# A residual made beside the first blocks and loaded back in the tail, and merge inputs by halves of tokens

## The chip, the cores and the metric

The kernel runs on one core of a Trainium2 chip. The metric is the device time of one execution in microseconds (us); the time quoted for a kernel is the median over its runs. A core has five engines with their own instruction lists: TensorE (PE, with its weight loads shown as PEld), VectorE (DVE), ScalarE (ACT), GpSimd (POOL) and SyncE (SP), which in this kernel only issues DMAs. SBUF is the on-chip memory, a bank is one of the eight PSUM banks into which TensorE writes.

## What is computed

One layer of a streaming encoder, all in fp32, for 1024 prompt tokens and 64 sample tokens (1088 in all) of width 1024. The rows of x are normalised, projected to 9864 columns, mixed by three branches (A: RWKV-7, B: mLSTM, C: stick-breaking attention), merged with gates, projected, normalised again and finished with a gated embedding. Cut to what matters here:

```python
x = layer_norm(x, ln_in_g, ln_in_b)
cols = x @ w_in + b_in
ys = stack([ya * silu(a_z), yb * silu(b_z), yc * silu(c_z)])
br = einsum('btnc,ncd->btnd', ys, w_branch)
mix = sum(sigmoid(gates) * br, axis=2) @ w_out
x = layer_norm(alpha * x + mix, ln_g, ln_b)      # alpha = 2 ** 0.25
x = x + (p @ w_ple) * sigmoid(x @ w_ple_gate)
```

The `alpha * x` of the last norm, with x the result of the first, is the residual that the change is about.

## The kernel before

Every fp32 operand of a large product is split into a high and a low part (`h`, `l`), and a product is three matmuls, h·h, h·l and l·h (`three`, called by `block`). Activations are kept transposed (channels on partitions, tokens along columns) in `xh` and `xl`, and the tokens come in three groups of 384, 384 and 320 columns.

**Stages.** `intro` loads nine tiles of x (128 tokens each, the last with 64), takes mean and variance of each row (`rs0`, `nmr0`), normalises the rows in place, and lets TensorE transpose them; the gain and bias `ln_in_g`, `ln_in_b` are applied to the transposed form. Its order is written out in the string `INTRO`. Then come the main blocks, one for each 128 columns of w_in: 8 pieces of the contraction x 3 matmuls x 3 token groups = 72 matmuls a block, some 12 us. The weights of a block are loaded by SP one or two blocks ahead (`wload`, L747) and split by ScalarE and VectorE one block ahead (`wsplit`; its subtraction reads the fp32 weights and their high part and shows as `whl<-heap,whl` of L358). At the end of a group VectorE and ScalarE empty the bank (`a_evac` for branch A: a shifted copy by ScalarE, one column of it by a POOL copy of L382, and a scalar-tensor step of VectorE). The three branches run as side tasks between these blocks. After the branches, `merge` multiplies their outputs with w_branch (its inputs, of 4 pieces, made by `yconv`: 4 x 3 matmuls for each of the three groups, 36 a block), and `tail` does the rest.

**What sets the order.** A planner, `Sched`, decides while the program is written out in which place of each engine's list an instruction stands. It keeps a simulated clock for each engine with costs given in `emit`, polls its tasks (lower priority numbers first) and puts a side task's instruction behind the main products that its clock says run until then. Each engine then executes its own list strictly in order and waits on semaphores. Side tasks are started with `S.spawn`.

**Branch A's front** (`a_front`, eight times, in two passes of 256 or 320 columns each) computes from three stored inputs the scaled keys and the norms of them. On VectorE it is a chain: tensor-scalar steps (L371), a scan (L401), products (L358) and scalar-tensor products (L376). At the end of a pass TensorE transposes the squares (`sq`) and multiplies with `bd`, a block-diagonal matrix of ones that sums over each head: the bd matmul. POOL's 128x128 memsets ahead of the fronts clear branch A's states.

**The tail.** For each of the nine token blocks TensorE does the products with w_out (8 pieces x 2 halves of 512 columns x 3 = 48 matmuls of 512 columns; 32 for the block of 64 tokens) and then, from the post norm `post`, 8 transposes of the normalised rows in two groups of 4. `post` on VectorE adds the residual tile to the two banks, takes statistics, and makes the normalised rows with two 128x1024 scalar-tensor steps (L376), between them a reciprocal square root by Newton steps on columns of 128x1. The residual tile comes from `res(t)`: SP loads x once more, POOL normalises it (L371) with `rs0` and `nmr0` and multiplies and adds two rows (L360) that `tail_rows` loaded on POOL's queue and VectorE scaled by alpha:

```python
yield self.dma(b, src, "s")
yield self.ts(b, b, self.rs0[:m, t:t + 1], OP.mult, nmr[:m, t:t + 1], OP.add, e="g")
yield self.tt(b, b, r3[:m, 0, :], OP.mult, "g")
yield self.tt(b, b, r3[:m, 1, :], OP.add, "g")
```

Beside this, VectorE splits the weights of the embedding (w_ple and w_ple_gate, loaded by SP; `heapr<-heap,heapr` 128x512 of L358), and the products of the embedding (`ple`) follow.

**The helpers' lines** in the profile: L321 a matmul, L328 a transpose on TensorE, L353 ScalarE, L358 and L360 a tensor-tensor step on VectorE and on POOL, L371 a tensor-scalar step, L376 a scalar-tensor-tensor step, L381 and L382 a copy on VectorE and on POOL, L401 the scan, L412 and L415 the statistics, L423 and L424 a memset on POOL and VectorE, L431 a DMA of a task, L747 the weight load. In the names, `heap` is the common SBUF pool (`heapr` the part that holds split operands), `bk` a bank, `pc` and `der` constants per channel.

## Time and profile before

| what | before |
|---|---|
| runs | 1802.21, 1797.72 and 1798.39 us, median 1798.39 |
| the profiled execution | 1793.48 us, its span 1791.5 us, granted TensorE clock 0.99 of full speed |
| TensorE busy | 1719.0 us (96% of the span), weight loads 1591.3 |
| VectorE busy | 1169.2 us (65%) |
| ScalarE busy | 790.8 us (44%) |
| POOL busy | 511.3 us (29%) |
| chain of work that ended last | TensorE 81%, VectorE 11%, ScalarE 4% |
| TensorE before its first product | some 33 us |
| longest waits of TensorE, whole run | transposes (L328) for VectorE L376: 22.1 us in 6; products (L321) for ScalarE L353: 15.0 us in 27; products for ScalarE's split in the merge: 5.7 us in 2 |

How to read it: busy time is the time in which an engine executed anything; an engine that is 96% busy leaves 72 us of the span. A line of a timeline gives the start, the duration, the engine, the line of the code, the operation, what is written from what, and in brackets the idle time of the engine just before it with what ended it. In a grouped line stand the count, the busy time, the mean duration in ns, and the idle time before these instructions. The runs without a profile lie 0.24 to 0.49% above the profiled execution.

### The profile page before, as it was taken

Reading aid. Unit: us, or ns where it says so; the run is one execution under the profiler, and the core shown is the slowest. Engines: PE = TensorE matmul, PEld = TensorE weight load, DVE = VectorE, ACT = ScalarE, POOL = GpSimd, SP = SyncE. Lnnn points to the kernel's source line nnn. Section 1 sums busy time; section 2 is a strip of 40 time slices with the busy share of each in tenths; the row PEclk is TensorE's granted clock in tenths of the full one; section 3 lists DMA queues with packets and bytes.
Section 4 is the critical chain, followed back from the end, with each engine's and each line's share of the span. In section 5 each row is a group of like instructions: output and inputs, shape, how many; then the busy total and the mean of one; then the engine's idle time right before and its main releaser. Section 6 shows DMA issues by size and latency. Waiting matters only on the chain.

```text
span 1791.5 us, 30062 instructions
## 1 busy us (share of the span) xinstructions
PE 1719.0 (96%) x10873; PEld 1591.3 (89%) x10873; DVE 1169.2 (65%) x2618; ACT 790.8 (44%) x1821; POOL 511.3 (29%) x1004
## 2 busy tenths in 40 slices
PE   6999999999999999999999999999998999978999
PEld 5999898888888999999999999999998999766787
DVE  8346567766766556777535757566664688888743
ACT  6444454445455455445436555554543223211421
POOL 6007554536645712321022112020210000354100
PEclk9999999999999999999999999999999999989999
DMA  5333331332332334543344342342326777321421
GB/s 156 100 102 93 96 103 54 111 104 67 94 103 72 91 106 147 160 138 122 114 128 141 98 121 94 90 130 71 109 64 193 240 254 232 129 71 59 143 83 53
DMA packets 223403, 207.64 MB, mean 116 GB/s; under 512 B 53396, under 2 KB 192454, under 8 KB 223254
## 3 DMA queue, kind: packets, MB, share of 16 engines
q1 hardware_dynamic: 195998, 163.99, 31.2%
q10 hardware_dynamic: 22552, 29.02, 4.5%
q0 software_dynamic: 4704, 12.71, 2.2%
q8 instruction: 85, 1.39, 0.3%
q14 instruction: 64, 0.52, 0.1%
HBM read 136.81 MB, written 68.90 MB: 115 GB/s over the span
## 4 chain that ended last, share of the span: by engine, by line
PE 81%; DVE 11%; ACT 4%; issue 2%; DMA 2%; ACTq 0%; SPq 0%; POOL 0%; DVEq 0%
PE bk L321 76%; PE bk L328 6%; DVE heap L376 4%; ACT heap L353 3%; DVE heap L358 2%; DVE heap L371 1%; DVE heapr L358 1%; DVE whl L358 1%; DVE heap L412 1%; DMA heap<-in_x_prompt_dram 1%; DVE xl L358 0%; DMA heap<-in_w_ple_dram 0%; DMA out_c_p_dram<-heap 0%; DVE heap L409 0%; ACT whl L353 0%
## 5 line engine op out<-in xcount | busy, mean ns | idle before, releaser
L321 PE MATMUL bk<-xh,whl 128*128 128x384 f32 (+3 forms) x3792 | 1056.7, 339 | 1.0 <-DVE xh L381 0.7
L321 PEld LDWEIGHTS bk<-xh,whl 128*128 128x128 f32 (+1 forms) x3792 | 681.1, 187 | 13.5 <-issue 3.9
L321 PE MATMUL bk<-xl,whl 128*128 128x384 f32 (+3 forms) x2184 | 669.2, 328 | 1.8 <-POOL xl L360 0.9
L321 PEld LDWEIGHTS bk<-xl,whl 128*128 128x128 f32 (+1 forms) x2184 | 404.0, 188 | 5.9 <-POOL xl L360 1.8
L353 ACT ACTIVATE heap<-bk 64x64 f32<-64x64 f32 (+9 forms) x679 | 219.2, 335 | 399.9 <-PE bk L321 137.8
L360 POOL TENSOR_TENSOR heap<-heap 32x30 f32<-32x30 f32 (+16 forms) x498 | 312.3, 627 | 37.3
L328 PE MATMUL bk<-ident,heap 128*128 128x128 f32 (+3 forms) x942 | 177.3, 280 | 36.4 <-DVE heap L376 22.1
L358 DVE TENSOR_TENSOR heap<-heap 128x256 f32<-128x256 f32 (+15 forms) x359 | 176.1, 497 | 16.2 <-DMA heap<-yz 7.8
L358 DVE TENSOR_TENSOR whl<-heap,whl 128x1024 fp32r<-128x1024 f32 (+1 forms) x114 | 121.7, 1069 | 91.2 <-ACT whl L353 87.9
L321 PE MATMUL bk<-heap 128*128 128x128 f32 (+6 forms) x1156 | 169.0, 270 | 10.0 <-ACT heap L353 8.5
L328 PEld LDWEIGHTS bk<-ident,heap 128*128 128x128 f32 (+3 forms) x942 | 120.7, 143 | 55.0 <-DVE heap L376 25.8
L321 PEld LDWEIGHTS bk<-heap 128*128 128x128 f32 (+2 forms) x1156 | 126.6, 163 | 40.6 <-ACT heap L353 21.9
L353 ACT ACTIVATE heap<-bk,pc 128x384 f32<-128x384 f32 (+5 forms) x218 | 114.1, 548 | 90.8 <-PE bk L321 69.2
L353 ACT ACTIVATE heap<-heap 64x64 f32<-64x64 f32 (+8 forms) x328 | 111.0, 343 | 63.4 <-DVE heap L376 30.5
L376 DVE SCALAR_TENSOR_TENSOR heap<-heap 128x4 f32<-128x4 f32 (+8 forms) x264 | 100.8, 383 | 55.3 <-ACT heap L353 49.6
L353 ACT ACTIVATE whl<-heap 128x1024 fp32r<-128x1024 f32 (+1 forms) x116 | 105.5, 911 | 70.7 <-PE bk L321 42.8
L401 DVE TENSOR_TENSOR_SCAN heap<-heap,cst 128x512 f32<-128x512 f32 (+8 forms) x68 | 96.4, 1419 | 45.5 <-POOL heap L418 26.1
L321 PE MATMUL bk<-heapr,whl 128*128 128x384 f32 (+2 forms) x648 | 117.2, 339 | 6.1 <-ACT heapr L353 5.7
L321 PEld LDWEIGHTS bk<-heapr,whl 128*128 128x128 f32 x648 | 110.2, 190 | 10.5 <-ACT heapr L353 6.3
L321 PE MATMUL bk<-heapr 128*128 128x256 f32 (+2 forms) x524 | 119.4, 329 | 0.0
L353 ACT ACTIVATE heap<-bk,hb 128x384 f32<-128x384 f32 (+1 forms) x120 | 67.7, 564 | 110.8 <-PE bk L321 87.8
L321 PE MATMUL bk<-heap,heap 128*128 128x128 f32 (+3 forms) x788 | 108.2, 263 | 8.3 <-ACT heap L353 6.5
(155 smaller groups left out, 1801.0 us busy)
## 6 DMA issues: line engine op xcount, KB each, us to landing
heap<-in_w_in_dram SPq DMA_DIRECT2D x77, 512.0 KB
heap<-gt SPq DMA_DIRECT2D x24, 544.0 KB
gt<-heap ACTq DMA_DIRECT2D x48, 192.0 KB
heap<-in_x_prompt_dram SPq DMA_DIRECT2D x16, 512.0 KB
heap<-crd SPq DMA_DIRECT2D x12, 544.0 KB
heap<-yd SPq DMA_DIRECT2D x24, 272.0 KB
heap<-yz SPq DMA_DIRECT2D x24, 272.0 KB
heap<-in_w_branch_dram SPq DMA_DIRECT2D x24, 256.0 KB
```

The costliest lines, as they stand in the source:

```text
L321: lambda: self.nc.tensor.matmul(out, lhsT, rhs, start=start, stop=stop, skip_group_check=more),
L328: lambda: self.nc.tensor.transpose(out, in_, self.ident[:p, :p]), load=(0.82 * fsize(in_), d))
L353: return self.nc.scalar.activation(out, in_, func, **kw)
L358: lambda: self.nc.vector.tensor_tensor(out=out, in0=a, in1=b, op=op))
L360: lambda: self.nc.gpsimd.tensor_tensor(out=out, in0=a, in1=b, op=op))
L371: lambda: q.tensor_scalar(out=out, in0=a, scalar1=s1, scalar2=s2, op0=op0, **kw))
L376: lambda: self.nc.vector.scalar_tensor_tensor(out=out, in0=a, scalar=s, in1=b, op0=op0, op1=op1))
L401: return self.S.emit("dve", fsize(out) * 2.13 + 90, rd, [out], lambda: self.nc.vector.tensor_tensor_scan(out=out, data0=d0, data1=d1, init ...
L412: return self.S.emit("dve", fsize(in_) * 1.06 + 65, [in_], [out], lambda: self.nc.vector.bn_stats(out=out, in_=in_))
```

## The change

A new task `resid` starts at the end of `intro` with priority 3. It keeps the nine tiles of normalised rows, loads `ln_in_g` and `ln_in_b` on SP, lets ScalarE scale them by alpha, and makes the residual in place with 18 POOL tensor-tensor steps; SP stores the nine tiles to DRAM (`resd`). In the tail `res` only loads such a tile, on SP; the second load of x, POOL's normalisation and its 18 steps there, two of the four rows and their scaling are gone. `yconv` converts the branch outputs in another order: the four pieces of the first 544 tokens first, then those of the second 544, for every merge (before: both halves of a piece, then the next piece). In `a_front` two memsets and one copy go from POOL to VectorE (24 small instructions in all).

```diff
--- before.py
+++ after.py
@@ -727,7 +727,24 @@
         for x in INTRO.split():
             if evs or x[0] not in "PEvW" and x[:2] != "w2":
                 f[x[0]](*(int(a) if a.isdigit() else a for a in x[1:]))
-        self.free(*xts, *tmps, bst)
+        self.free(*tmps, bst)
+        self.S.spawn(self.resid(xts), "resid", 3)
+
+    def resid(self, xts):
+
+        self.resd = self.dr.tile([9, 128, 1024], F32, name="resd")
+        R = yield from self.get(2048)
+        r3 = R.v(2, 1024)
+        for j, nm in enumerate(("ln_in_g", "ln_in_b")):
+            yield self.dma(r3[:, j, :], self.I[nm].rearrange("(a b) -> a b", a=1).to_broadcast([128, 1024]), "s")
+        for j in range(2):
+            yield self.act(r3[:, j, :], r3[:, j, :], AF.Copy, scale=2.0 ** 0.25)
+        for t, x in enumerate(xts):
+            m = 128 if t < 8 else 64
+            for j, op in enumerate((OP.mult, OP.add)):
+                yield self.tt(x[:m, :1024], x[:m, :1024], r3[:m, j, :], op, "g")
+            yield self.dma(self.resd[t, :m], x[:m, :1024], "s")
+        self.free(R, *xts)
 
 
     def wsetup(self, specs):
@@ -1022,7 +1039,7 @@
 
         h3, l3 = self.ys[n]
         H = NT // 2
-        it = [(k, slice(o, o + H)) for k in range(4) for o in (0, H)]
+        it = [(k, slice(o, o + H)) for o in (0, H) for k in range(4)]
         bs = []
         for _ in range(4):
             bs.append((yield from self.get(H)))
@@ -1115,13 +1132,10 @@
         self.wod = True
 
     def tail_rows(self):
-        rows = yield from self.get(4096)
-        r3 = rows.v(4, 1024)
-        for j, nm in enumerate(("ln_in_g", "ln_in_b", "ln_g", "ln_b")):
-            a = self.I[nm].rearrange("(a b) -> a b", a=1) if j < 2 else self.I[nm]
-            yield self.dma(r3[:, j, :], a.to_broadcast([128, 1024]))
-        for j in range(2):
-            yield self.ts(r3[:, j, :], r3[:, j, :], 2.0 ** 0.25, OP.mult)
+        rows = yield from self.get(2048)
+        r3 = rows.v(2, 1024)
+        for j, nm in enumerate(("ln_g", "ln_b")):
+            yield self.dma(r3[:, j, :], self.I[nm].to_broadcast([128, 1024]))
         self.rows = rows
 
     def tok(self, t):
@@ -1132,7 +1146,7 @@
         self.free(*self.Wr)
         self.banks += self.mbanks
         yield lambda: self.rows is not None
-        r3 = self.rows.v(4, 1024)
+        r3 = self.rows.v(2, 1024)
         mx = self.mix.v(8, NT)
         fl = lambda x: x.rearrange("p a b -> p (a b)")
         k3 = lambda x, c=128: x.rearrange("p (k c) -> p k c", c=c)
@@ -1146,18 +1160,13 @@
         hls = [[k3(wf[:, 2048 + 1024 * j:3072 + 1024 * j]) for j in range(2)]]
         hls += [[x[:, :, 512 + 128 * i:640 + 128 * i] for x in self.wo] for i in range(2)]
         self.x2d = self.dr.tile([9, 128, 1024], F32, name="x2d")
-        nmr = self.nmr0
         order = [0, 1, 2, 3, 4, 5, 6, 8, 7]
         sz = lambda t: 128 if t < 8 else 64
 
         def res(t):
-            m, src = self.tok(t)
+            m = sz(t)
             x = yield from self.get(1024)
-            b = x[:m, :1024]
-            yield self.dma(b, src, "s")
-            yield self.ts(b, b, self.rs0[:m, t:t + 1], OP.mult, nmr[:m, t:t + 1], OP.add, e="g")
-            yield self.tt(b, b, r3[:m, 0, :], OP.mult, "g")
-            yield self.tt(b, b, r3[:m, 1, :], OP.add, "g")
+            yield self.dma(x[:m, :1024], self.resd[t, :m], "s")
             self.res[t] = x
             if t < 8:
                 self.S.spawn(res(t + 1), "res")
@@ -1195,9 +1204,9 @@
                 yield self.bns(s[:m, 6 * h:6 * h + 6], r[:m, c])
                 self.unbank(bks[h])
             yield self.bna(s[:m, 12:14], s[:m, 0:12])
-            yield self.stt(r[:m, :1024], r[:m, :1024], s[:m, 12:13], r3[:m, 2, :], OP.subtract, OP.mult)
+            yield self.stt(r[:m, :1024], r[:m, :1024], s[:m, 12:13], r3[:m, 0, :], OP.subtract, OP.mult)
             yield from self.rsqrt(s[:m, 14:15], s[:m, 13:14], s[:m, 15:16], 1e-5)
-            yield self.stt(r[:m, :1024], r[:m, :1024], s[:m, 14:15], r3[:m, 3, :], OP.mult, OP.add)
+            yield self.stt(r[:m, :1024], r[:m, :1024], s[:m, 14:15], r3[:m, 1, :], OP.mult, OP.add)
             yield self.dma(self.x2d[t, :m], r[:m, :1024], "s")
             for k0 in (0, 4):
                 b = yield from self.bank()
@@ -1360,8 +1369,8 @@
         PC = yield from self.get(nc)
         bk3, kr3, pt3, ns3 = BK.v(nc, 128), KR.v(nc, 128), Pt.v(nc, 65), NS.v(nc, 2)
         nsb = NS[:, 2 * nc:3 * nc]
-        yield self.memset(pt3[:, :, 0], 1.0)
-        yield self.memset(ns3[64:128], 1.0)
+        yield self.memset(pt3[:, :, 0], 1.0, "v")
+        yield self.memset(ns3[64:128], 1.0, "v")
         yield
         w0, a0, kk, ka, rk = (self.pcol(n, p) for n in ("w0_a", "a0_a", "k_k", "k_a", "r_k"))
         lw = self.lw[:, p * 128:(p + 1) * 128]
@@ -1432,7 +1441,7 @@
             self.unbank(b1)
             self.unbank(b2)
             yield
-        yield self.cp(PC[:, :nc], pt3[:, :, 64], "g")
+        yield self.cp(PC[:, :nc], pt3[:, :, 64])
         self.free(*T, xk, xr, Pt)
         self.afdone = 2 * p + hf + 1
         self.S.note(f"   scores {p}{hf}")
```

Three places in the lists of the engines, before and after the change (a row that ends in x3 stands for three like instructions in a row; numbers of buffers are left out, and `heap_76` is a second part of the heap).

POOL, behind `intro`, beside the main blocks of branch A, before the change:

```order
L382 COPY heap<-der 128x1 x3
L423 MEMSET heap 128x128 x4
L423 MEMSET heap 128x1024
L382 COPY heap<-der 128x1 x4
L423 MEMSET heap 128x8
L423 MEMSET heap 64x16
L382 COPY heap<-der 128x1 x4
L382 COPY heap<-heap 128x8
```

And with the change:

```order
L423 MEMSET heap_76 128x1024
L360 TENSOR_TENSOR heap<-heap,heap_76 128x1024 x2
L382 COPY heap<-der 128x1 x2
L360 TENSOR_TENSOR heap<-heap,heap_76 128x1024 x5
L382 COPY heap<-der 128x1 x2
L360 TENSOR_TENSOR heap<-heap,heap_76 128x1024 x5
L382 COPY heap<-der 128x1 x2
L360 TENSOR_TENSOR heap<-heap,heap_76 128x1024 x4
L360 TENSOR_TENSOR heap<-heap,heap_76 64x1024
L382 COPY heap<-der 128x1 x2
L360 TENSOR_TENSOR heap<-heap,heap_76 64x1024
L382 COPY heap<-der 128x1 x4
```

The 18 steps now stand in one run behind the memsets, and between them only the one-column copies of the evacuations of two main blocks.

VectorE, the first pass of branch A's first front, before the change (ahead of these rows stand the tensor-scalar and the scan that begin the pass; the rows that read a bank or write `whl` belong to the main blocks):

```order
L371 TENSOR_SCALAR heap<-heap,der 128x256 x2
L358 TENSOR_TENSOR heap<-heap 128x256
L376 SCALAR_TENSOR_TENSOR heap<-bk_66,der,heap 128x384
L358 TENSOR_TENSOR heap<-heap 128x4x64 x2
L376 SCALAR_TENSOR_TENSOR heap<-heap,pc 128x2x128
L358 TENSOR_TENSOR heap<-heap 128x2x2x64
L376 SCALAR_TENSOR_TENSOR heap<-heap,pc 128x2x64
L376 SCALAR_TENSOR_TENSOR heap<-bk_67,der,heap 128x256
L376 SCALAR_TENSOR_TENSOR heap<-bk_67,der,heap 128x64
L376 SCALAR_TENSOR_TENSOR heap<-heap,pc 128x2x64
L358 TENSOR_TENSOR whl<-heap,whl 128x1024
```

And with the change, again behind that tensor-scalar and that scan:

```order
L371 TENSOR_SCALAR heap_76<-heap_76,der 128x256
L376 SCALAR_TENSOR_TENSOR heap<-bk_66,der,heap 128x384
L371 TENSOR_SCALAR heap_76<-heap_76,der 128x256
L358 TENSOR_TENSOR heap_76<-heap_76 128x256
L358 TENSOR_TENSOR heap_76<-heap_76 128x4x64 x2
L376 SCALAR_TENSOR_TENSOR heap_76<-heap_76,pc 128x2x128
L376 SCALAR_TENSOR_TENSOR heap<-bk_67,der,heap 128x256
L376 SCALAR_TENSOR_TENSOR heap<-bk_67,der,heap 128x64
L358 TENSOR_TENSOR whl<-heap,whl 128x1024
L376 SCALAR_TENSOR_TENSOR heap<-bk_65,der,heap 128x384
L358 TENSOR_TENSOR heap_76<-heap_76 128x2x2x64
L376 SCALAR_TENSOR_TENSOR heap_76<-heap_76,pc 128x2x64 x2
```

The evacuations and the weight split of the main blocks now stand ahead of the last three steps of the pass; on TensorE the transposes of the squares stand behind 402 main products instead of 366, and the bd matmul behind 405 instead of 375.

SP, the first loads of the tail, before the change:

```order
L431 DMA heap<-in_p_prompt_dram 128x256 x4
L431 DMA heap<-in_x_prompt_dram 128x1024
L431 DMA heap<-in_w_ple_dram 128x512 x2
L431 DMA heap<-in_p_prompt_dram 128x256 x2
L431 DMA heap<-in_w_ple_gate_dram 128x512 x2
L431 DMA heap<-in_x_prompt_dram 128x1024
L431 DMA heap<-in_w_ple_gate_dram 128x512 x4
L431 DMA x2d<-heap 128x1024
```

And with the change:

```order
L431 DMA heap<-in_p_prompt_dram 128x256 x4
L431 DMA heap<-in_w_ple_dram 128x512 x2
L431 DMA heap<-resd 128x1024 x2
L431 DMA heap<-in_p_prompt_dram 128x256
L431 DMA heap<-resd 128x1024 x2
L431 DMA heap<-in_p_prompt_dram 128x256
L431 DMA heap<-in_w_ple_gate_dram 128x512 x6
L431 DMA x2d<-heap 128x1024
L431 DMA heap<-resd 128x1024
```

Four tiles of the residual are loaded ahead of the first weights of the gate, where one tile of x stood. In TensorE's list of the tail the first transposes of the post norm stand behind 105, 147, 192, 237, 288, 333 and 386 products for blocks 0 to 6 (before: 120, 150, 216, 258, 291, 333 and 381), counted from the tail's first product.

## Rows read from the trace of the kernel before

**Rows 1.** (lines grouped by form, TensorE, 1524.2 to 1658.7 us): busy us, mean ns | idle before

```profile
L321 PE MATMUL bk<-xh,heapr 128*128 128x512 f32 x272 | 94.5, 415 | 0.0
L321 PE MATMUL bk<-xl,heapr 128*128 128x512 f32 x144 | 59.0, 410 | 0.0
L328 PE MATMUL bk<-ident,heap 128*128 128x128 f32 x60 | 12.6, 344 | 22.1 <-DVE heap L376 22.1
```

**Rows 2.** (timeline of TensorE, tail): start us, us, engine, line, op [idle before]

```profile
1540.23 0.39 PE L321 MATMUL bk<-xl,heapr 128*128 128x512 f32 x1
...
1551.90 0.39 PE L321 MATMUL bk<-xl,heapr 128*128 128x512 f32 x1
...
1556.54 1.12 PE L328 MATMUL bk<-ident,heap 128*128 128x128 f32 x4 [4.02 <-DVE heap L376]
...
1565.85 0.60 PE L328 MATMUL bk<-ident,heap 128*128 128x128 f32 x4
1566.20 0.48 PE L321 MATMUL bk<-xh,heapr 128*128 128x512 f32 x1
```

**Rows 3.** (windows): us, PE PEld DVE ACT POOL busy (x), PEclk, DMA share, GB/s

```profile
1582.00:1594.40 12.40, 5.98 (x20) 4.94 (x20) 11.81 (x23) 1.29 (x3) 4.20 (x2) 0.72 0.10 42
```

**Rows 4.** (lines grouped by form, POOL, 1500 to 1700 us)

```profile
L360 POOL TENSOR_TENSOR heap<-heap 128x1024 f32<-128x1024 f32 x16 | 42.7, 2671 | 1.3
...
L360 POOL TENSOR_TENSOR heap<-heap 64x1024 f32<-64x1024 f32 x2 | 4.9, 2434 | 0.2
```

**Rows 5.** (timeline of POOL: start of the run, and tail)

```profile
39.74 0.99 POOL L360 TENSOR_TENSOR xl<-heap,xh 128x320 fp32r<-128x320 f32 x1 [3.35 <-DVE xh L381]
...
1543.85 6.06 POOL L360 TENSOR_TENSOR heap<-heap 128x1024 f32<-128x1024 f32 x2
...
1599.09 5.14 POOL L360 TENSOR_TENSOR heap<-heap 128x1024 f32<-128x1024 f32 x2
```

**Rows 6.** (timeline of VectorE, tail)

```profile
1544.45 3.20 DVE L376 SCALAR_TENSOR_TENSOR heap<-heap 128x1024 f32<-128x1024 f32 x1
1547.57 2.89 DVE L358 TENSOR_TENSOR heapr<-heap,heapr 128x512 fp32r<-128x512 f32 x1
...
1550.94 0.16 DVE L376 SCALAR_TENSOR_TENSOR heap<-heap 128x1 f32<-128x1 f32 x1
...
1551.21 0.69 DVE L358 TENSOR_TENSOR heapr<-heap,heapr 128x512 fp32r<-128x512 f32 x1
...
1555.21 1.28 DVE L376 SCALAR_TENSOR_TENSOR heap<-heap 128x1024 f32<-128x1024 f32 x1
...
1601.75 0.68 DVE L358 TENSOR_TENSOR heap<-bk,heap 128x512 f32<-128x512 f32 x1
```

**Rows 7.** (timeline of SP's queue: the third weight load of the main blocks)

```profile
51.82 0.37 SPq L747 DMA_DIRECT2D heap<-in_w_in_dram  x1
```

**Rows 8.** (DMA issues, tail): out<-in, queue, count, KB each, us to landing

```profile
heap<-in_ln_in_b_dram POOLq DMA_DIRECT2D x1, 512.0 KB, 5.2
```

**Rows 9.** (timeline of ScalarE, start of the merge)

```profile
1382.95 0.66 ACT L353 ACTIVATE heapr<-heap 128x544 fp32r<-128x544 f32 x1 [1.75 <-DVE heap L376]
```

**Rows 10.** (timeline of VectorE: intro, and the first front of branch A)

```profile
39.04 0.55 DVE L381 CAST xh<-heap 128x320 fp32r<-128x320 f32 x2
39.91 1.00 DVE L381 CAST xh<-heap 128x320 fp32r<-128x320 f32 x1
...
83.94 0.30 DVE L371 TENSOR_SCALAR heap<-heap 128x256 f32<-128x256 f32 x1 [1.07 <-ACT heap L353]
...
91.40 0.34 DVE L376 SCALAR_TENSOR_TENSOR heap<-heap,pc 128x128 f32<-128x128 f32 x1
```

**Rows 11.** (timeline of TensorE, first front of branch A)

```profile
92.39 0.59 PE L321 MATMUL bk<-heap,bd 128*128 128x256 f32 x2
...
97.60 0.70 PE L321 MATMUL bk<-heap 64*128 64x256 f32 x4
```

**Rows 12.** (timeline of TensorE, start of the merge)

```profile
1381.26 0.69 PE L321 MATMUL bk<-heapr,whl 128*128 128x384 f32 x1 [5.06 <-ACT heapr L353]
```

## Prediction

> **What bounds the kernel now.** I read the busy times of the page first (the table ahead): TensorE is busy 1719.0 of 1791.5 us, so only about 72 us of the span can be won without taking products away. Then the waits of TensorE, to see where those 72 lie: the first 33 us (nothing loaded yet), some 20 us in small pieces inside branch A, 6 us where the merge begins, and the tail. The tail is the largest and the only one that one cause explains. From its first product at 1524.27 to the first product of the embedding at 1658.73 TensorE issues 272 + 144 = 416 products of 512 columns and 60 transposes, and the transposes stood waiting for VectorE for 22.1 us [rows 1]. The reader is to see in the timeline of TensorE what dense work costs there: between two like products at 1540.23 and 1551.90 lie 51 products, 0.229 us each, and four transposes take 0.35 us (1565.85 to 1566.20) [rows 2]. 416 x 0.229 + 60 x 0.0875 = 100.5 us; the stretch lasted 134.5. So 34.0 us are lost: 22.1 of waiting, 11.9 of slow running behind the waits, where four transposes take 1.12 us and not 0.60 (1556.54 against 1565.85) [rows 2]; the granted clock, 0.99 over the whole run (the table), is 0.72 over the longest wait and its wake [rows 3], a mean of the two levels 1.2 and 2.4 GHz.
>
> Why VectorE is late there: beside the chain of each block (residual add, statistics, two 1024-wide steps, Newton steps) POOL makes the residual: for each block a normalisation and two products of 128x1024, which took 2.67 us [rows 4]; a multiply and an add alike are called a product here. While a product runs, a VectorE instruction with two inputs in SBUF does not run: the 128x1024 step took 3.20 us and a 128x512 subtraction 2.89 us under the pair of products at 1543.85 [rows 5, 6], together 4.1 us over the 1.28 and 0.69 that they take at 1555.21 and 1551.21 [rows 6], and the transposes behind them waited 4.02 us [rows 2]. An add that reads a bank and one SBUF tile took 0.68 under the pair at 1599.09 [rows 5, 6]: it is not held. One such VectorE instruction gets through per POOL product, no more.
>
> **Part 1, the residual leaves the tail.** Removed there: nine x loads, 9 POOL normalisations, 18 POOL products, two row loads, two VectorE scalings. Added: nine loads of the stored residual on SP, of the same size. SP now has four of them ahead of the w_ple_gate loads (the order of SP, ahead), where one x tile stood before; 1.5 MB more ahead of the first gate weights is covered, since those weights are first used after product 416, some 90 us later. Without POOL all the holding goes. The change also has transposes earlier in TensorE's list (block 0 after 105 products instead of 120, block 2 after 192 instead of 216); the undisturbed chain of a block is some 8 us of VectorE time (four 512-wide steps at 0.7, two 1024-wide at 1.28, some fifteen small ones at 0.16 [rows 6]), two splits per block run between, and the transposes stand 45 to 57 products, 10 to 13 us, behind their block, so what is late next is VectorE by a little. I allow 3 us of new waits (0 at best; 12 if the earlier places and the splits of weights that share VectorE cost half of what was won). Gain: 34.0 - 3 = **31 us** (22 to 34).
>
> **Part 2, the residual is made early.** The same 18 products now run on POOL behind the first memsets. When: the two rows are loaded by SP behind the third weight load, issued at 51.82 [rows 7], and one store, so at about 52.6 and 53.0; landing took 5.2 us for such a row [rows 8], ACT takes 0.66 for 544 columns [rows 9], so about 1.1 for a row; the first product starts near 59.5. Bare, a product is 2.43 us, the 64-row form, which was hardly disturbed [rows 4]. By 84 nine are done, with two weight splits held by 2 us each; a split runs most of a block ahead of its use and has that room. Then VectorE comes to the first front of branch A. In the order of VectorE, ahead, twelve of its instructions, up to the last product for the bd matmul, are of the kind that shares with POOL: nine with two SBUF inputs (one scan, four products, three scalar-tensor products, one weight split) and three tensor-scalars from SBUF to SBUF. Before, this chain ran from 83.94 to 91.74 [rows 10]. Now each waits for the POOL product in hand. I follow the list: tensor-scalar at 86.6, scan 89.3, tensor-scalar 92.4, evacuation 92.7, tensor-scalar 95.3, products 98.0, 100.8 and 103.6, scalar-tensor product 106.2; then an evacuation, the weight split (POOL's next copy waits for VectorE here, so it is not held), an evacuation, and the last product and two scalar-tensor products under the last POOL product: done at about 112.6. TensorE's list has the bd matmul 30 products later than before, which is just behind the second pair of front products, 97.60 in the old trace (the old bd matmul stood at 92.39) [rows 11]; less the matmul itself that is 97.5. It waits 112.6 - 97.5 = 15.1 us, and runs slowly behind it; 11.9 us over six waits, most of it behind the four long ones, makes 2.5 for one. Cost: **17.6 us**.
>
> Does the kind without a second SBUF input, the tensor-scalar, wait at all? A cast of that kind, SBUF to SBUF, took 1.00 us with POOL's product of 39.74 beside it, two others together 0.55 [rows 5, 10], so I count it in. The Trainium skill ("SBUF — State Buffer", Who interferes with whom) says more: copies, casts and tensor-scalars can take both ports and are then held, instructions with at most one SBUF input outside that mode are not. The trace agrees on the cast and on the bank-reading add; no row shows a tensor-scalar of this size under a POOL product. Without the three the chain would end at 107.9, the wait be 10.4 and the cost 12.9: the low end by rows; at the very best POOL's products fall where TensorE has room and it is 2 us. The high end is the tail's own price for 18 such products, 34 us.
>
> What else moves early: nine 512 KB stores on SP. A store waits for its POOL product, and behind it in SP's list stand stores of branch A's inputs and the weight loads. By the times above SP is held 1 to 5 us, while a weight is loaded a block (72 products, some 12 us) before its split: covered. POOL's one-column copies for the evacuations stand behind up to five products, 12 us, which is the block by which they run ahead; if they come 2 us late, TensorE has two more banks, 8 us. 24 memsets and copies go from POOL to VectorE, 0.1 to 0.3 us each, under the cover of TensorE: nothing. The nine kept tiles and the two rows hold 11,264 columns of the heap longer, so buffers change places; TensorE's list runs equal again some 640 block products on and stays within two dozen products of the old one until the tail.
>
> **Part 3, halves.** Before, TensorE waited 5.06 us for the seventh piece and went on at 1381.26 [rows 12]. Now the first group needs pieces 1 to 4 and starts without a wait, but the second group straddles both halves and needs piece 8, whose ACT copy ran at 1382.95 to 1383.61 [rows 9], its subtraction to 1384.4. Old: 27 products of the first block behind 1381.26; new: 15 behind 1384.4. At 0.17 us each that is 1385.9 against 1386.9; at half speed 1390 against 1389.5. I take **-0.5 us** (-2 to +1).
>
> **Sum.** -31 + 17.6 - 0.5 = -13.9. The profiled execution took 1793.48 us, 1779.6 after; it lies 4.9 under the median of the three, 1798.39, so I give 1798.4 - 13.9 = **1784.5 us**. A measurement here can tell about 0.3%, 5.4 us, from no change.
>
> **Rivals.**
> *Early is nearly free* (22%): VectorE reaches the front after POOL is through, or the holding falls into TensorE's room. For: an evacuation that is late by less than two groups of TensorE costs nothing. Against: nine products are still left at 84, and the bd matmul waits for the chain itself. The early cost is then 2 to 9, the time 1768 to 1776.
> *The tail pays only in part* (16%): the chains of the blocks stay late, by the earlier places of the transposes, and 12 us of waits return; with the early cost as summed or somewhat larger the change is within 0.3%, 1793 to 1803. That no part works as said is in this case too; against it stands that each wait in the tail has a held VectorE step just ahead.
> *Slower* (11%): one mechanism, POOL's list itself. Its one-column copies wait for VectorE, VectorE waits for its products, and SP's weight loads stand behind the stores that wait for POOL. If this ring makes the last product end after about 134 and not 112, the bd matmul waits 36 us and the early cost passes the tail's gain: 1804 to 1812. Against: the ring closes only at one place (ahead of the last product), and 22 us of VectorE's time would have to go.
> *Forecast* (51%): early 10 to 22, tail 27 to 33: 1777 to 1793.
>
> Range: from 1768, the free early place with a full tail, to 1797, where the second rival is cut in its middle; about 6% lie below, 14% above. Faster by over 0.3%: 0.51 + 0.22 = 0.73; within: 0.16; slower: 0.11.
>
> **What would show it.** In the profile after: no POOL product behind 1500 and the waits of transposes for VectorE in the tail down from 22.1 to some 3; 18 POOL products from 59 to 112, two-input VectorE instructions of 2.5 to 3 us between 85 and 112; one wait of TensorE of 10 to 15 us near 98, at the bd matmul, with a low clock behind it; at the merge two or three short waits in place of 5.06. If that one wait is missing, the early step is wrong; if transposes still wait 10 us in the tail, the first.

## The result and the profile after

The changed kernel takes 1766.79 us (median of 4 runs, 1764.83 to 1767.26) against 1798.06 of the kernel before (4 runs of the same job): the ratio is 0.9822, 95% interval 0.9802 to 0.9842, so it is 31 us faster, and 17.7 us faster than the 1784.5 that I forecast, just outside the range. Its profiled execution took 1766.90 us, 26.6 less than that of before (1793.48). Lines of its page, the clock's line of the page of before, and TensorE's waits after:

```profile
span 1765.1 us, 30061 instructions
...
PE 1711.2 (97%) x10873; PEld 1587.3 (90%) x10873; DVE 1154.9 (65%) x2640; ACT 792.6 (45%) x1823; POOL 493.6 (28%) x969
...
PEclk9989999999999999999999999999999999999999
```

```profile
PEclk9999999999999999999999999999999999989999
```

```profile
PE bk L321 <- DVE heap L376: 14.6, 6, 11.8
PE bk L321 <- ACT heap L353: 14.2, 27, 1.6
PE bk L328 <- ACT heap L353: 12.1, 2, 10.4
PE bk L321 <- ACT heapr L353: 4.0, 3, 1.7
```

(Waits: us in total, times, longest.) The transposes' wait for VectorE, 22.1 us before, is gone from the list, and a new wait of 11.8 us stands at its head. The low digit of the granted clock has moved from the tail to the third of the 40 slices of the span, around 100 us.

**The tail.** Grouped lines of TensorE from the first product with w_out, 1532.01, to the first of the embedding, 1634.13, and one row of VectorE:

```profile
L321 PE MATMUL bk<-xh,heapr 128*128 128x512 f32 x272 | 89.3, 397 | 0.0
L321 PE MATMUL bk<-xl,heapr 128*128 128x512 f32 x144 | 56.6, 393 | 0.0
L328 PE MATMUL bk<-ident,heap 128*128 128x128 f32 x60 | 9.1, 272 | 0.0
```

```profile
1548.67 1.28 DVE L376 SCALAR_TENSOR_TENSOR heap<-heap 128x1024 f32<-128x1024 f32 x1
```

The same instructions as in [rows 1] now last 102.1 us where they took 134.3 (1524.41 to 1658.75), without any wait and at a granted clock of 1.00, before 0.91. The 128x1024 step that took 3.20 us under POOL's pair [rows 6] takes 1.28.

**The first front.** VectorE, POOL and TensorE (start, duration, engine, line, operation):

```profile
84.87 1.95 DVE L371 TENSOR_SCALAR heap<-heap 128x256 f32<-128x256 f32 x1 [1.98 <-ACT heap L353]
86.85 2.77 DVE L401 TENSOR_TENSOR_SCAN heap<-cmask,heap 128x256 f32<-128x256 f32 x1
89.54 2.45 DVE L371 TENSOR_SCALAR heap<-heap,der 128x256 f32<-128x256 f32 x1
91.92 0.61 DVE L376 SCALAR_TENSOR_TENSOR heap<-bk,der,heap 128x384 f32<-128x384 f32 x1
...
94.59 5.44 DVE L358 TENSOR_TENSOR heap<-heap 128x256 f32<-128x256 f32 x3
99.97 2.55 DVE L376 SCALAR_TENSOR_TENSOR heap<-heap,pc 128x256 f32<-128x256 f32 x1
...
106.25 0.41 DVE L358 TENSOR_TENSOR heap<-heap 128x256 f32<-128x256 f32 x1
106.70 2.71 DVE L376 SCALAR_TENSOR_TENSOR heap<-heap,pc 128x128 f32<-128x128 f32 x2
```

```profile
60.09 4.93 POOL L360 TENSOR_TENSOR heap<-heap,heap 128x1024 f32<-128x1024 f32 x2 [6.31 <-ACT heap L353]
...
92.11 12.60 POOL L360 TENSOR_TENSOR heap<-heap,heap 128x1024 f32<-128x1024 f32 x5
...
106.66 2.33 POOL L360 TENSOR_TENSOR heap<-heap,heap 64x1024 f32<-64x1024 f32 x1
```

```profile
109.46 1.22 PE L321 MATMUL bk<-heap,bd 128*128 128x256 f32 x2 [11.82 <-DVE heap L376]
```

Of the VectorE instructions that POOL holds, one gets through per POOL step. The exceptions are the first of the three products at 94.59, which took 0.41 us at the seam of two POOL steps, and the product at 106.25, which meets POOL's copies, 0.41. The evacuation at 91.92, which reads a bank, takes its usual 0.61. The weight split took 2.77 us here (103.03), 1.23 before.

**The start of the merge**, which answers to [rows 12]:

```profile
1380.87 2.43 PE L321 MATMUL bk<-heapr,whl 128*128 128x384 f32 x13
...
1385.27 0.45 PE L321 MATMUL bk<-heapr,whl 128*128 128x384 f32 x1 [1.18 <-ACT heapr L353]
...
1388.34 1.77 PE L321 MATMUL bk<-heapr,whl 128*128 128x384 f32 x3 [1.69 <-ACT heapr L353]
1391.21 2.04 PE L321 MATMUL bk<-heapr,whl 128*128 128x384 f32 x4 [1.10 <-ACT heapr L353]
```

The first group's 12 products run through; the second group waits for the pieces of the second half one by one, three short waits in place of 5.06 us.

**Along the run.** The start of the same TensorE product in both profiled executions, read from the two traces (main products are those with the columns of w_in, counted from the first):

```
after so many main products     before     after    difference
400                               97.2      96.4      -0.8
800                              175.5     190.3     +14.8
1200                             283.7     292.8      +9.1
2400                             630.9     639.4      +8.5
first product of the merge      1373.0    1380.9      +7.9
first product with w_out        1524.4    1532.0      +7.6
first product of the embedding  1658.8    1634.1     -24.6
last matmul, end                1787.1    1760.9     -26.2
```

So the kernel is 14.8 us late behind the early step, 5.7 of them come back between the main products 800 and 1200 and 1.2 more up to the merge, the tail gains 32.2, and the stretch behind it 1.5.

### The profile page after: what moved, and what is told of

It reads as the page before. It is cut to its first block, busy times and chain, and to the rows that moved or that the text cites. A ratio compares the mean times of both kernels' runs of the same rounds, so it can differ in the third digit from the quotient of the medians.

```text
span 1765.1 us, 30061 instructions
## 1 busy us (share of the span) xinstructions
PE 1711.2 (97%) x10873; PEld 1587.3 (90%) x10873; DVE 1154.9 (65%) x2640; ACT 792.6 (45%) x1823; POOL 493.6 (28%) x969
## 4 chain that ended last, share of the span: by engine, by line
PE 83%; DVE 9%; ACT 4%; issue 2%; DMA 1%; POOL 0%; ACTq 0%; SPq 0%; DVEq 0%; POOLq 0%
PE bk L321 78%; PE bk L328 5%; DVE heap L376 3%; ACT heap L353 3%; DVE heap L358 2%; DVE heap L371 2%; DVE whl L358 1%; DMA heap<-yz 1%; DMA heap<-in_x_prompt_dram 1%; ACT whl L353 0%; DVE heap L412 0%; DVE xl L358 0%; ACTq L431 0%; DVE heap L381 0%; DVE heap L409 0%
## 5 line engine op out<-in xcount | busy, mean ns | idle before, releaser
L321 PEld LDWEIGHTS bk<-xh,whl 128*128 128x128 f32 (+1 forms) x3792 | 682.1, 188 | 12.3 <-issue 3.4
L360 POOL TENSOR_TENSOR heap<-heap 32x30 f32<-32x30 f32 (+14 forms) x480 | 267.9, 558 | 36.3
L358 DVE TENSOR_TENSOR heap<-heap 128x256 f32<-128x256 f32 (+16 forms) x352 | 168.0, 483 | 11.8 <-DMA heap<-yz 3.4
L321 PE MATMUL bk<-heap 128*128 128x128 f32 (+7 forms) x886 | 157.6, 293 | 8.7 <-ACT heap L353 7.8
L321 PEld LDWEIGHTS bk<-heap 128*128 128x128 f32 (+3 forms) x886 | 117.8, 182 | 30.7 <-ACT heap L353 19.9
L353 ACT ACTIVATE heap<-heap 64x64 f32<-64x64 f32 (+10 forms) x330 | 113.1, 347 | 45.4 <-DVE heap L376 18.4
L321 PE MATMUL bk<-heap,heap 32*32 32x32 f32 (+3 forms) x1058 | 125.7, 244 | 6.9 <-ACT heap L353 6.4
L321 PEld LDWEIGHTS bk<-heap,heap 128*128 128x128 f32 (+2 forms) x1058 | 98.7, 152 | 31.7 <-ACT heap L353 17.6
L321 PEld LDWEIGHTS bk<-heapr,whl 128*128 128x128 f32 x648 | 110.0, 191 | 10.4 <-ACT heapr L353 5.1
```

What stands on the lines that cost most here:

```text
L321: lambda: self.nc.tensor.matmul(out, lhsT, rhs, start=start, stop=stop, skip_group_check=more),
L353: return self.nc.scalar.activation(out, in_, func, **kw)
L358: lambda: self.nc.vector.tensor_tensor(out=out, in0=a, in1=b, op=op))
L360: lambda: self.nc.gpsimd.tensor_tensor(out=out, in0=a, in1=b, op=op))
```

## The experiments

**The early steps left out, in place.** The kernel leaves out the 18 POOL steps; every other row of every list stays where it was.

```diff
-                           lambda: self.nc.gpsimd.tensor_tensor(out=out, in0=a, in1=b, op=op))
+                           lambda: e == "g" and self.nc.gpsimd.tensor_tensor(out=out, in0=a, in1=b, op=op))
...
-                yield self.tt(x[:m, :1024], x[:m, :1024], r3[:m, j, :], op, "g")
+                yield self.tt(x[:m, :1024], x[:m, :1024], r3[:m, j, :], op, "n")
```

> The changed kernel without the 18 early POOL steps; every other instruction keeps its place in its engine's list (the stored residual is the normalised x alone). Theory (POOL's steps hold VectorE, and only in the first front): the wait of 11.8 us at the bd matmul near 98 us is gone, the two-input VectorE steps there take 0.3 to 0.7 us instead of 2.5, and the time falls from 1766.8 by the whole 14.5 us by which the run with the change is late at 150 us, to about 1752. Rival 1 (a late TensorE is partly paid back inside branch A, since the branch's chains then stand ready: 6 us came back between 220 and 370 us): without the delay those 6 us are lost again, and the time is about 1758. Rival 2 (the stores and ScalarE's scaling cost, not the steps): the wait stays and the time is 1765 to 1768.

1754.04 us (1752.82 to 1755.47). The scan of the first front, and the bd matmul, now without a wait:

```profile
86.23 0.69 DVE L401 TENSOR_TENSOR_SCAN heap<-cmask,heap 128x256 f32<-128x256 f32 x1
```

```profile
98.51 0.59 PE L321 MATMUL bk<-heap,bd 128*128 128x256 f32 x2
```

Against the changed kernel it is 13.65 us ahead at main product 800, still 13.6 at 1200, 12.3 at 2000 and 11.4 at the end. So the steps alone make the loss, 13.65 us, and only some 2 us of it come back further on. The 5.7 us between 800 and 1200 are another thing: this kernel has no delay at all, stands 1.2 us behind the kernel before at product 800 and 4.5 ahead of it at 1200. Rival 1 falls for most of the 6 us, rival 2 altogether.

**The residual alone**, merge order and the 24 small instructions as before:

```diff
-        it = [(k, slice(o, o + H)) for o in (0, H) for k in range(4)]
+        it = [(k, slice(o, o + H)) for k in range(4) for o in (0, H)]
...
-        yield self.memset(pt3[:, :, 0], 1.0, "v")
-        yield self.memset(ns3[64:128], 1.0, "v")
+        yield self.memset(pt3[:, :, 0], 1.0)
+        yield self.memset(ns3[64:128], 1.0)
...
-        yield self.cp(PC[:, :nc], pt3[:, :, 64])
+        yield self.cp(PC[:, :nc], pt3[:, :, 64], "g")
```

> The changed kernel with the merge inputs in the old order and the 24 small instructions of the fronts back on POOL; TensorE's list is that of the change but for a few places. Theory (the 6 us that come back between 220 and 370 us come from the other order of branch A's work, which the new task causes): 1767, the halves worth 0.3 us. Rival (they come from the small instructions, which left POOL's list): 1772 to 1774.

1768.74 us (1767.77 to 1768.97). At product 1200 it stands 1.1 us ahead of the changed kernel, so the small instructions bring nothing; the 5.7 us come with the order of branch A's work that the new task causes. Between the first product of the merge and the first with w_out it takes 151.65 us, the changed kernel 151.14.

**Branch A's inverses left out in both kernels, in place.** Which work of the other order is it? In the kernel before, the front of VectorE at 259 to 275 us lies beside POOL's inverse, 60 dependent steps that grow from 32x30 to 32x240 and shrink again, the longest in its middle (a grouped line names the form of its first step alone; "32x30 and smaller" in the expectation below is a misreading of it). POOL up to 276 us and three of VectorE's steps there, in the kernel before:

```profile
254.55 21.72 POOL L360 TENSOR_TENSOR heap<-heap 32x30 f32<-32x30 f32 x33
```

```profile
262.52 1.31 DVE L358 TENSOR_TENSOR heap<-heap 128x256 f32<-128x256 f32 x2
...
268.91 0.76 DVE L376 SCALAR_TENSOR_TENSOR heap<-heap,pc,heap 128x128 f32<-128x128 f32 x1
```

And in the changed kernel, POOL up to 300 us:

```profile
273.67 26.36 POOL L360 TENSOR_TENSOR heap<-heap 32x30 f32<-32x30 f32 x38
```

```profile
275.71 0.43 DVE L358 TENSOR_TENSOR heap<-heap 128x256 f32<-128x256 f32 x1
...
280.12 0.34 DVE L376 SCALAR_TENSOR_TENSOR heap<-heap,pc,heap 128x128 f32<-128x128 f32 x1
```

In the kernel before POOL starts 5 us ahead of the front (its scan stands at 259.98), which so meets the middle of the inverse; with the change both start together (POOL at 273.67, the scan at 273.79), and the first steps of the inverse are the short ones. That lessens the holding and does not end it: the second 128x128 step (280.94) still takes 0.60 us, and from the scan to that step's end VectorE needs 10.4 us before (259.98 to 270.37) and 7.7 after (273.79 to 281.54). TensorE's waits beside it, before (200 to 290 us) and after (210 to 300):

```profile
PE bk L321 <- ACT heap L353: 2.6, 5, 1.1
PE bk L321 <- DVE heap L386: 1.4, 2, 0.9
PE bk L328 <- DVE heap L358: 1.1, 1, 1.1
PE bk L321 <- DVE heap L376: 1.0, 1, 1.0
```

```profile
PE bk L321 <- ACT heap L353: 3.3, 6, 1.4
PE bk L328 <- DVE heap L358: 0.6, 1, 0.6
PE bk L321 <- DVE heap L371: 0.3, 1, 0.3
PE bk L321 <- DVE heap L376: 0.2, 1, 0.2
```

The waits for VectorE fall from 3.5 to 1.1 us. From main product 800 to 1200, 740 matmuls in either kernel, TensorE waits 4.9 us before and 2.2 after and runs at a granted clock of 0.98 and 1.00: of the 5.7 us 2.7 are waits, the rest is slower running.

The cut, `IE = "g"` to `IE = "n"` with the line of the first diff, in both kernels:

> The kernel before without the 480 small POOL steps (32x30 and smaller) of branch A's inverses, every other instruction in its place (the branch's inverse is left out). To be read beside the same cut of the changed kernel. Theory (the 5.6 us that the changed order wins between the main products 800 and 1200 are VectorE steps of branch A's front that no longer lie under POOL's small steps): the 128x256 steps near 262 us take 0.4 us and not 0.65 to 1.3, this kernel is 5 us or more ahead of the kernel before at main product 1200 (283.7 us), and the run with the change and this cut is 14 to 15 us behind this one there. Rival (the order wins it in another way, without POOL): the difference to the run with the change stays 9 us at product 1200.

> The changed kernel with the same cut, the 480 small POOL steps of the inverses left out in place. Theory: it loses 14 to 15 us against the cut kernel before up to main product 600 and still is 14 to 15 us behind at product 1200, so nothing comes back; its time is that of the cut kernel before less about 20 us. Rival: 9 us behind at product 1200, and the time less 25 us.

1770.60 us (2 runs) and 1750.37 (2 runs). Main product 1200 starts at 274.7 in the first, 9.0 ahead of the kernel before, and the difference between the two cut kernels is 13.8 us at product 800, 13.5 at 1200, 13.6 at 2400, 13.1 at the merge: next to nothing comes back. The time differs by 20.2 us. The theory holds. The same steps of VectorE in the cut kernel before:

```profile
259.05 0.76 DVE L358 TENSOR_TENSOR heap<-heap 128x256 f32<-128x256 f32 x2
...
262.69 0.34 DVE L376 SCALAR_TENSOR_TENSOR heap<-heap,pc,heap 128x128 f32<-128x128 f32 x1
```

It also leaves out the inverses' own time: TensorE's waits between 140 and 620 us fall from some 20 us to 5.1, and which part of that is holding was not separated. What the two cuts show is that the 5.7 us hang on the inverses.

**The tail's steps left out of the kernel before, in place** (`"n"` with the line of the first diff).

```diff
-            yield self.tt(b, b, r3[:m, 0, :], OP.mult, "g")
-            yield self.tt(b, b, r3[:m, 1, :], OP.add, "g")
+            yield self.tt(b, b, r3[:m, 0, :], OP.mult, "n")
+            yield self.tt(b, b, r3[:m, 1, :], OP.add, "n")
```

> The kernel before without the 18 POOL steps of the tail; loads, POOL's normalisation and all other places stay (the residual is the normalised x alone). Theory (the steps hold VectorE, nothing else in the tail matters): the transposes' waits for VectorE fall from 22.1 us to under 4, the half-speed stretches of the tail go, and the time is 1798 - 30, about 1768. Rival (the transposes' place in TensorE's list, or the loads of x and the normalisation, carry a good part): 8 us or more of waits stay, and the time is 1777 to 1790.

1760.84 us (1760.60 to 1761.42). With w_out it takes 102.3 us, the changed kernel 102.1. The loads of x and POOL's normalisations are still there, and no transpose waits:

```profile
L328 PE MATMUL bk<-ident,heap 128*128 128x128 f32 x61 | 9.5, 273 | 0.0
```

```profile
L371 POOL TENSOR_SCALAR heap<-heap,rs,nmr 128x1024 f32<-128x1024 f32 x8 | 12.2, 1522 | 73.6 <-DMA heap<-in_x_prompt_dram 55.0 <-DMA heap<-in_w_ple_dram 13.2 <-DVE heap L371 5.3
```

So the 18 steps are the whole loss of the tail; removing the loads and the normalisations, and the transposes' new places, give nothing that shows in the time. It came out 7 us under what I expected, 5 of them since the kernel before took 1793.22 us (13 runs) beside it and not 1798: to that the difference is 32.4 us, ratio 0.9826, interval 0.9800 to 0.9852.

**The kernel before once more.**

> The kernel before, profiled once more. Theory (the 4.9 us by which its profiled execution lay under the median are chance of that execution): the new profiled execution lies within 3 us of the median of the runs, 1795 to 1801, and the difference to the old one is in the tail's waits. Rival (a profiled execution of this kernel is some 5 us shorter always): 1791 to 1795 again.

1792.20 us over 10 runs, 1787.11 to 1800.00, the profiled one 1795.90, now 3.7 us above the median. A difference in the tail's waits was expected and did not show: 22.4 us beside 22.1. The 4.9 us were chance. The two profiles of the kernel before differ behind the tail, from the first product of the embedding to the last matmul: 128.3 us at a granted clock of 1.00 in the first, 131.3 at 0.97 in the second. The kernel before spreads over 13 us in these 10 runs, the kernel without POOL's tail steps over 0.8 in 4.

**The steps on VectorE.** First by the task's own call, so that the planner counts them there:

```diff
-                yield self.tt(x[:m, :1024], x[:m, :1024], r3[:m, j, :], op, "g")
+                yield self.tt(x[:m, :1024], x[:m, :1024], r3[:m, j, :], op)
```

> The changed kernel with the 18 early steps on VectorE instead of POOL. A 128x1024 step with two inputs takes VectorE 1.28 us where nothing holds it: 23 us in all, beside 10 of its 40 us in use between 45 and 84 us. Theory (only the holding by POOL costs, VectorE has room): the wait at the first bd matmul falls from 11.8 us to under 3, and the time lies between that without the steps, 1754, and 1760, so 7 to 12 us under the changed kernel. Rival (VectorE itself becomes late for the first front, some 8 of the steps stand among its work, or the other order of branch A loses its 5 us): 1762 to 1768.

1771.20 us (1769.82 to 1773.06), 4 more than the changed kernel and outside both ranges. At product 800 it is 14.4 us ahead of it, as hoped; at the first product of the merge 9.1 ahead, at the first with w_out 3.2 behind. The planner has another order, by which branch C ends later: TensorE is ahead and branch C is not. SP's queue stores its last output at 1365.60 us and the merge begins at 1371.78, 6.2 us later; in the changed kernel 1363.09 and 1380.87. The loads of the merge's inputs stand behind that store in SP's list, and TensorE waits for ScalarE's copies of them (9.8 us in 7, the changed kernel 4.0 in 3):

```profile
1365.60 0.45 SPq L431 DMA_DIRECT2D yd<-heap  x1
1366.21 0.46 SPq L431 DMA_DIRECT2D heap<-yd  x1
```

```profile
PE bk L321 <- ACT heapr L353: 9.8, 7, 2.3
```

Then by the planner's old count, so that the lists of TensorE, ScalarE and SP are the change's:

```diff
-                           lambda: self.nc.gpsimd.tensor_tensor(out=out, in0=a, in1=b, op=op))
+                           lambda: (self.nc.gpsimd if e == "g" else self.nc.vector).tensor_tensor(out=out, in0=a, in1=b, op=op))
...
-                yield self.tt(x[:m, :1024], x[:m, :1024], r3[:m, j, :], op, "g")
+                yield self.tt(x[:m, :1024], x[:m, :1024], r3[:m, j, :], op, "p")
```

> The changed kernel with the 18 early steps given to VectorE in the places at which they were called for POOL: the lists of TensorE, ScalarE and SP are those of the change to the last row, VectorE's has 18 rows more, POOL's 18 fewer. Five of them (1.28 us each) stand inside the first front's chain up to the last product for the bd matmul, eleven ahead of it. Theory (the cost of the early steps is POOL's holding, and the version on VectorE before lost its gain at the merge by another order of branch C): the wait at the first bd matmul is under 4 us, the merge begins as in the change, and the time is 1754 to 1759. Rival (VectorE has no room in the first front): the wait stays above 8 us and the time is 1762 or more.

1753.23 us (1753.09 to 1754.49), as fast as without the steps; the changed kernel took 1767.36 beside it. VectorE and the bd matmul (L360 is the line of POOL's call, here given to VectorE):

```profile
85.62 0.69 DVE L401 TENSOR_TENSOR_SCAN heap<-cmask,heap 128x256 f32<-128x256 f32 x1
...
88.03 1.22 DVE L360 TENSOR_TENSOR heap<-heap,heap 128x1024 f32<-128x1024 f32 x1
89.17 0.88 DVE L358 TENSOR_TENSOR heap<-heap 128x256 f32<-128x256 f32 x2
```

```profile
97.70 0.70 PE L321 MATMUL bk<-heap,bd 128*128 128x256 f32 x2
```

A step costs VectorE 1.22 us; waiting for one of POOL's cost an instruction of this chain some 2 us (the scan 2.77 instead of 0.69). The wait at the bd matmul is gone.

**A third pair of buffers for the merge's inputs**, on top of that:

```diff
-        for _ in range(4):
+        for _ in range(6):
...
-        yield from load_y(0)
+        for i in range(2):
+            yield from load_y(i)
...
-            if i < 7:
-                yield from load_y(i + 1)
+            if i < 6:
+                yield from load_y(i + 2)
```

(and `i % 3` for `i % 2` in the choice of a pair.)

> As the version with the 18 steps in place on VectorE, and the merge's inputs loaded through three pairs of buffers instead of two, so two pieces ahead. Theory (at the start of the merge each piece waits for its load, which waits for a buffer that the piece two before it gives free: the order of the halves moves the waits, the depth removes them): TensorE's waits for ScalarE at the merge, 4.0 us in 3, and the 6.8 us at half speed behind them fall to under half, and the time is 4 to 7 us below that version. Rival (the loads are bound by the DMA engines or by the last store of branch C, not by the buffers): within 2 us of that version.

1751.82 us (1751.40 to 1754.04): 2.1 us of the merge gained in the profiled execution, 1.4 in the medians. That is the rival's size, not the 4 to 7 us of the theory. The waits for ScalarE there, 4.2 us in 3 without the third pair:

```profile
PE bk L321 <- ACT heapr L353: 2.6, 3, 1.1
```

The depth takes a third of the waits and not all; what holds the rest was not followed. Its median is the lowest here, 0.977 of the kernel before, interval 0.9749 to 0.9792, but its runs and interval overlap with those of the version before it (0.9756 to 0.9798).

**The halves alone.**

```diff
-        it = [(k, slice(o, o + H)) for k in range(4) for o in (0, H)]
+        it = [(k, slice(o, o + H)) for o in (0, H) for k in range(4)]
```

> The kernel before with the merge's inputs by halves of tokens and nothing else. Theory: between the first product of the merge and the first with w_out TensorE needs 0.3 to 0.6 us less, two or three waits in place of the one of 5.06 us; the time cannot be told from that of the kernel before. Rival (three short waits cost more than a long one by the clock): 1 us or more longer in that stretch.

1795.64 us against 1794.18, ratio 1.001 (0.999 to 1.003). From the first product of the merge to the first with w_out it takes 151.44 us, the kernel before 151.43 and, in its second profile, 151.79. The waits are as foreseen, three short ones in place of one, and the gain is 0 to 0.5 us (the 0.5 from the residual alone, 151.65, to the whole change, 151.14): too small to tell.

**The inverses on VectorE**, `IE = "v"` in the changed kernel:

> The changed kernel with the 480 small steps of the inverses on VectorE instead of POOL. Theory (POOL's small steps hold VectorE longer than VectorE would take for them): TensorE's waits between 140 and 620 us, 16.5 us in the changed kernel, fall by a third or more, 1757 to 1763. Rival (the chain of VectorE in branch A is the limit, and it gets some 80 us more of work there): 1767 to 1780.

1813.25 us (2 runs), above both ranges. Not for the reason of the rival: the planner's other order lets TensorE run up to 50 us ahead in main products while the side tasks stay behind, and what is left of them stands ahead of the merge, whose inputs then come late:

```profile
PE bk L321 <- ACT heapr L353: 22.1, 17, 6.7
```

So the question whether VectorE would make these steps cheaper stays open.

**The changed kernel once more.**

> The changed kernel once more, on the chip of these runs, so that the versions are compared with it there. Theory: 1764 to 1769, a spread of some 3 us where the kernel before spreads over 10 or more, since the tail's waits, which POOL's steps set by chance, are gone. Rival (the spread belongs to the chip): as wide as that of the kernel before.

1767.36 us, 1765.92 to 1769.26, beside 1794.18 (1787.21 to 1797.82): ratio 0.9856, interval 0.9830 to 0.9882. The spread goes with the tail's POOL steps, as far as 4 runs tell. It is not seen in the tail's waits, as the theory had it: they were 22.1 and 22.4 us in two executions that differ by 2.4 us. How it comes about stays open.

## Why the prediction was wrong, step by step

| step | predicted | measured |
|---|---|---|
| tail, part 1 | -31 | -32.2 |
| first front, part 2 | +17.6 | +14.8 |
| from main product 800 to the merge | 0 | -6.9 |
| merge, part 3 | -0.5 | -0.3 |
| behind the tail | 0 | -1.5 |
| profiled execution to profiled execution | -13.9 | -26.6 |
| from the profiled execution to the median | +4.9 | -0.1 |

(The rest of the measured 26.6, some 0.4 us, lies behind TensorE's last matmul and outside the span.)

**Part 1 was right**, in its mechanism and nearly in its size. Waits of 22.1 and slow running of 11.9 us were to go but for 3; no wait stayed. The dense work was counted 1.6 us too short, though: without a wait and at a granted clock of 1.00 the stretch takes 102.1 us, not 100.5, so the slow running was some 10 us. (The first product with w_out starts at 1524.41, not 1524.27; the stretch before is 134.3 us.) The kernel before with the steps left out shows that they were the cause.

**Part 2 was right where it looked.** POOL's steps ran from 60.1 to 109.0 (forecast 59.5 to some 112), the chain of VectorE ended at 109.4 (112.6), the wait was 11.8 (15.1) and the slow running behind it 14.5 - 11.8 = 2.7 (2.5; 14.5 is the difference at main product 450, the first behind the front in both). The tensor-scalars were held, as I had counted them: 1.95, 2.45 and 2.23 us in this front, where the kernel without the steps needs 0.30, 0.39 and 0.34. That agrees with the Trainium skill ("SBUF — State Buffer", Who interferes with whom), by which a tensor-scalar can take both of VectorE's port pairs and is then held by POOL; no row of before could show it at this size. The 3 us too many come from the product that slipped through at the seam of two POOL steps (94.59): the chain was at the end of its first scalar-tensor product at 102.5, forecast 106.2. Behind it I had two instructions the wrong way round, and the errors cancel by luck: the weight split was held (2.77 us), which I had ruled out, and the product at 106.25, which I had under the last POOL step, was not. By the kernel with the early steps left out their price is 13.65 us.

**What failed is the sentence that closed part 2**: that TensorE's list "runs equal again some 640 block products on", taken as nothing gained or lost on the way; 6.9 of the 12.7 us by which the forecast for the profiled execution was short lie there. I compared the order of TensorE alone. Between the main products 800 and 1200 the same instructions lie otherwise against POOL's inverses, and 5.7 us that VectorE's being held there had cost, the mechanism that I had found at both ends of the kernel, fell away. With the inverses cut out of both kernels there is nothing to fall away: the difference stays at 13.8 and 13.5 us. The 20 us of small waits in branch A stood in the first paragraph of the prediction, and I never asked who made them. Of the 6.9 us that came back up to the merge, 4.9 are there without any delay (the kernel with the early steps left out goes from 1.2 us behind the kernel before to 3.7 ahead of it); the other 2.0 come back only behind a delay (13.65 to 11.6 us), 1.2 of them between the products 1800 and 2000 and 0.9 between 4200 and 4400, and how was not followed up. The 1.5 us behind the tail, put at nothing too, are not chance: the stretch takes 126.8 us in all eight profiles with the whole change in them, 128.3 in the first profile of the kernel before, in the one without the inverses and in the one without the tail's steps, where one product waits 0.8 us for a subtraction of VectorE, and 128.3 with the residual alone, without that wait. What makes it was not followed.

**The second error is the 4.9 us.** The profiled execution of before lay under the median by chance, and I carried the difference to the changed kernel as if it were a constant. Without it the forecast would have been 1779.6, the range 1763 to 1792, and the measured time inside, by the width of the range and not by the mechanism. It shows in the measured gain as well: 31 us against the four runs of the first comparison, 26.8 against 13 other runs of the kernel before (1794.18 to 1767.36).

One reading of before is wrong without bearing on the sum: TensorE's first product starts at 15.42 us, not at some 33; of the first 45 us it is idle for 15.6.

The rival *early is nearly free* gave the nearest time, 1768 to 1776, by the wrong road: the early step was not free, it was paid and partly given back elsewhere. The rivals in which the tail pays only in part, and POOL's list closes a ring, did not occur; at the one place where the ring could close, POOL waited 0.55 us for VectorE and a product went through beside its copies.

## What to carry to other kernels

When a step is moved from one end of a kernel to the other, its price is set by what the neighbour engine needs at the new place: here 18 POOL steps cost 32 us in the tail and 13.7 near the start, and none that shows on VectorE itself, in the same places. That POOL is idle does not make work on it free; look for the VectorE steps with two operands in SBUF, and the tensor-scalars, that lie beside it, in every stretch where the order changes, also where the list of the bound engine reads the same. And a profiled execution's distance to the median is noise until a second profile shows it.

## What the runs showed of the hardware that I had not expected

Small POOL steps on 32 partitions hold a 128-partition VectorE step as the large ones do: beside the middle of an inverse a 128x256 product took 0.65 us and a 128x128 scalar-tensor product 0.76, without the inverse 0.38 and 0.34. And the steps of POOL with a constant per row instead of a second tensor hold VectorE too, for less time: in the kernel without the tail's steps eight 128x1024 tensor-scalars, 1.52 us each, stayed in the tail, and beside four of them a 128x512 subtraction of the embedding's weight split took 1.26 to 1.58 us (1.44 at 1538.31) instead of 0.68. No transpose waited for it, and the tail ran at its full speed. So it is what stands behind the held instruction that makes the price.
